# Attention scores as three products of rounded halves in place of one float32 product, with k split where it is transposed and q split tile by tile

## The chip, the cores and the metric

The kernel runs on one core of a Trainium2 chip. The metric is the device time of one execution in microseconds, as the median of several runs of the same program. The core has a matrix engine (PE, with its weight loads shown apart as PEld), three engines for elementwise work (DVE, ACT, POOL), and SP, which here only issues DMAs. Each engine works through its own list of instructions strictly in the order in which the program wrote them; engines wait for one another by semaphores.

## The reference

One encoder block over 1024 tokens of width 1024. The input projection feeds two groups: a gated depthwise convolution of 31 taps, and attention over a grid of 16 rows by 64 columns in which each query sees a clamped window of 8 rows by 16 columns. Then come an output projection, a residual, and a SwiGLU feed-forward network (FFN) with a residual. The change touches the scores alone:

```python
q = rms_norm(q.reshape(B, S, N_HEADS, HEAD_DIM), q_norm_g[l])   # 8 heads of 64
k = rms_norm(k.reshape(B, S, N_HEADS, HEAD_DIM), k_norm_g[l])
...
s = jnp.einsum("bqhd,brqchd->bhqrc", q_r, k_win,
               preferred_element_type=jnp.float32) * scale
s = s + bias
p = jax.nn.softmax(s, axis=(-2, -1))
```

## The kernel before

Almost every large matrix product is made from rounded halves. A float32 tile is split into a high part, its value rounded to a shorter mantissa (type `float32r`), and a low part, the difference. `split` writes the high part with a copy on ACT and the low part with a subtraction on another engine, by default POOL (lines 103 to 108). `mac` then adds three matmuls, high times high, high times low and low times high (lines 110 to 114). The attention is the exception: its scores (line 611), the transposes of the weights (642) and the products with v (658) are plain float32 matmuls.

The program is written out in the order in which each engine shall work. `weave` lets small pieces of work be written between the matmuls of a product, and `pump` writes convolution taps to DVE (line 319, some 1.3 us each) between other steps.

**The k stage.** `nat(1, t)` projects 128 tokens to k in the PSUM tile `z1t`. `head_post` follows it one step later: squares on ACT, then on DVE some taps, the reciprocal (line 380), the scaled copy `zn1t` (line 382), and one more tap. `head_T(1, t)` is written after the eighth triple of matmuls of the next projection: four transposes on PE (line 389), which read `zn1t`, then one ACT copy into `kT`, scaled by the norm's gain (line 396). So DVE has nothing to do for `kT` before the change. For tile 5 three taps more than usual stand ahead of the reciprocal (line 423). q goes the same way later, into `qT`.

**The attention loop** (lines 785 to 812) has 32 iterations for scores, each for a pair of heads of one tile of 128 queries; four in a row share a tile. The two heads of a pair lie in partitions 0 to 63 and 64 to 127 of `qT` and `kT`. Iterations 0 to 15 have windows of 288 keys, 16 to 31 windows of 384. In iteration i PE gets the scores of i (`score_mm`, tile `s`), the transposes of i - 2 (`flip`, tile `p`) and the product with v of i - 3 (`weigh`, tile `o`). DVE adds the bias and takes the maximum (624), ACT makes the exponentials and their sum (626), DVE the reciprocal (631). POOL scales the row of weights of iteration i - 1 (`score_norm`, line 633), which `flip` needs one iteration later. ACT and DVE copy the transposed weights out of the single PSUM buffer `p` (647). In eight iterations (16, 17, 20, 21, 24, 25, 28, 29) a quarter of an output weight is split as well, by an ACT copy (line 104) and a POOL subtraction (108), at the iteration's end; these are called jobs below. Iterations 0 and 1 lie between the last projections of v, beside the end of the convolution.

SBUF tiles come from pools with a fixed number of buffers: `H` holds six tiles of 16 KB per partition, `ST` five of 2 KB, `SM` sixteen small ones.

Of the kernel before, what the change touches and what calls it, by code (L numbers as in the profile page):

```python
# [6 lines left out]
F32 = mybir.dt.float32  # L7
F32R = mybir.dt.float32r
AF = mybir.ActivationFunctionType
OP = mybir.AluOpType  # L10
PSUM = bass.MemoryType.PSUM

P = 128
D = 1024
S = 1024
# [3 lines left out]
HD = 64  # L19
# [5 lines left out]
GW = 64  # L25
AR = 12
# [41 lines left out]
def build(ctx, tc, a):  # L68
    nc = tc.nc
    pe, act, dve, pool = nc.tensor, nc.scalar, nc.vector, nc.gpsimd  # L70
# [5 lines left out]
    def T(tag, shape, bufs, name, dt=F32):  # L76
        return sb.tile(shape, dt, tag=tag, bufs=bufs, name=name)
# [5 lines left out]
        return T("R", [P, 1024], 3, name)  # L83

    def H(name, dt=F32):
        return T("H", [P, 4096], 6, name, dt)

    def ST(name, dt=F32):
        return T("st", [P, 512], 5, name, dt)

    def SM(name, n=8):
        return T("sm", [P, 8], 16, name)[:, :n]

    def mm(name):
        return ps.tile([P, 512], F32, tag="mm", bufs=4, name=name)

    def tp(name):
        return ps.tile([P, 512], F32, tag="tp", bufs=2, name=name)
# [4 lines left out]
    def split(hi, lo, src, sub=(pool,)):  # L103
        act.copy(hi, src)  # L104
        n = src.shape[-1] // len(sub)
        for i, eng in enumerate(sub):
            sl = slice(i * n, (i + 1) * n)
            eng.tensor_tensor(*[w[..., sl] for w in (lo, src, hi.bitcast(F32))], OP.subtract)  # L108
# [47 lines left out]
    def take_parts(jobs, n=4, sub=pool):  # L156
        i = pos[1]
        hi, lo = chunks[i][2]()
        w = 1024 // n

        def part(o):
            sl = slice(o, o + w)
            split(hi[:, sl], lo[:, sl], raws[i][:, sl], (sub,))
            if o + w == 1024:
                raws.pop(i)
                issue()
        pos[1] += 1
        jobs.extend(lambda o=o: part(o) for o in range(0, 1024, w))
# [62 lines left out]
    qg, kg = par[:, 144:145], par[:, 145:146]  # L231
# [124 lines left out]
    def pump(n):  # L356
        for _ in range(n):
            if not next(conv, False):
                return


    qT, kT = H("qT").rearrange("p (c s) -> p c s", s=S), H("kT").rearrange("p (c s) -> p c s", s=S)

    def head_sq(n, t, z):
        sq, ss = ST(f"sq{n}{t}"), SM(f"s{n}{t}")
# [20 lines left out]
    def head_T(n, t, zn):  # L386
        pt = tp(f"zt{n}{t}")
        for c in range(4):
            pe.transpose(pt[:, c * P:(c + 1) * P], zn[:, c * P:(c + 1) * P], ident)
        if n == 0:  # L390
            q5 = qT.rearrange("p c (h b i j) -> p c h b i j", h=2, b=4, j=16)
            p5 = pt.rearrange("p (c i b j) -> p c i b j", c=4, i=2, j=16)
            for i in range(2):
                act.activation(q5[:, :, t // 4, :, 2 * (t % 4) + i, :], p5[:, :, i], AF.Copy, scale=qgs)
        else:
            act.activation(kT[:, :, t * P:(t + 1) * P], pt.rearrange("p (c s) -> p c s", s=P), AF.Copy, scale=kg)

    vd = dr.tile([S, 512], F32, name="vd")

# [175 lines left out]
    def table(rh, ty):  # L575
        n = AR * t1[ty].shape[-1]
        src = tf[rh, ty].rearrange("i j h c -> (i j) (h c)")
        if rh == 0 and ty == 0:
            parts = [(G(f"tab{k}")[:, :n * min(3, NH - 3 * k)], 3 * k) for k in range(3)]
        else:  # L580
            parts = [(H(f"tab{rh}{ty}")[:, :NH * n], 0)]
        heads = []
        for w, h0 in parts:
            nc.sync.dma_start(w, src[:, h0 * n:h0 * n + w.shape[-1]])
            heads += [w[:, o:o + n] for o in range(0, w.shape[-1], n)]
        return heads
# [4 lines left out]
    def load_vw(cb, g):  # L591
        c0, ncol, _ = WIN[cb]
        if g % 2 == 0:
            vwt[cb, g // 2] = G(f"vw{cb}{g}").rearrange("p (g d) -> p g d", d=512)
        vw[cb, g] = vwt[cb, g // 2][:4 * ncol, g % 2, :]
        nc.sync.dma_start(vw[cb, g], vd.rearrange("(r c) d -> r c d", c=GW)[g * 4:g * 4 + 4, c0:c0 + ncol, :])


    k4 = kT.rearrange("p c (r w) -> p c r w", w=GW)
    order = [(rh, cb) for cb in (0, 3, 1, 2) for rh in range(2)]  # L600
    tab, es, pTs, os_, at, sums, pp = {}, {}, {}, {}, {}, {}, {}

    def score_mm(i):
        s_, hp = divmod(i, 4)
        rh, cb = order[s_]
        t = rh * 4 + cb
        c0, ncol, _ = WIN[cb]
        out = []
        for hh in range(2):
            s = mm(f"s{i}{hh}")[:, :AR * ncol]  # L610
            pe.matmul(s, qT[hh * HD:(hh + 1) * HD, hp, t * P:(t + 1) * P],  # L611
                      k4[hh * HD:(hh + 1) * HD, hp, rh * 4:rh * 4 + AR, c0:c0 + ncol], start=True, stop=True)
            out.append(s)
        return out

    def score_exp(i, ss):
        s_, hp = divmod(i, 4)
        rh, cb = order[s_]
        n = AR * WIN[cb][1]
        e = es[i] = G(f"e{i}").rearrange("p (h n) -> p h n", h=2)[:, :, :n]  # L620
        rs = SM(f"rs{i}", 2)
        for hh in range(2):
            mx = SM(f"mx{i}{hh}", 1)
            dve.tensor_tensor_reduce(out=e[:, hh], in0=ss[hh], in1=tab[rh, cb][2 * hp + hh], scale=-1.0,  # L624
                                     scalar=3.0e38, op0=OP.add, op1=OP.min, accum_out=mx)
            act.activation(e[:, hh], e[:, hh], AF.Exp, bias=mx, scale=-1.0, accum_out=rs[:, hh:hh + 1])  # L626
        sums[i] = rs

    def score_norm(i):
        rs = sums.pop(i)  # L630
        dve.reciprocal(rs, rs)  # L631
        for hh in range(2):
            pool.tensor_scalar(es[i][:, hh], es[i][:, hh], rs[:, hh:hh + 1], 1.0, op0=OP.mult, op1=OP.mult)  # L633

    def flip(i):
        s_, hp = divmod(i, 4)
        m = 4 * WIN[order[s_][1]][1]
        pp[i] = cv(f"p{i}")
        for hh in range(2):
            pt = pp[i][:, hh * 512:hh * 512 + 384]  # L640
            for g in range(3):
                pe.transpose(pt[:m, g * P:(g + 1) * P], es[i][:, hh, g * m:(g + 1) * m], ident)  # L642
        pTs[i] = G(f"pT{i}").rearrange("p (n h q) -> p n h q", h=2, q=P)[:m, :3]

    def flip_out(i, hh):
        m = pTs[i].shape[0]
        (dve.tensor_copy, act.copy)[hh](pTs[i][:, :, hh], pp[i][:m, hh * 512:hh * 512 + 384].rearrange(  # L647
            "p (n q) -> p n q", q=P))

    def weigh(i):  # L650
        s_, hp = divmod(i, 4)
        rh, cb = order[s_]
        if hp == 0:
            os_[s_] = tp(f"o{s_}").rearrange("p (c q) -> p c q", c=4)
        for g in range(3):
            for hh in range(2):
                c = (2 * hp + hh) * HD
                pe.matmul(os_[s_][hh * HD:(hh + 1) * HD, hp], vw[cb, rh + g][:, c:c + HD], pTs[i][:, g, hh],  # L658
                          start=g == 0, stop=g == 2)

    def evac_hi(s_):
        rh, cb = order[s_]
        if rh == 0:
            at[cb] = [G(f"at{cb}{w}", F32R).rearrange("p (c t q) -> p c t q", c=4, t=2) for w in range(2)]
        act.copy(at[cb][0][:, :, rh], os_[s_])
# [12 lines left out]
    def load_window(cb):  # L678
        for g in range(4):
            load_vw(cb, g)  # L680

    for t in range(6):
# [5 lines left out]
        if t == 3:  # L688
            tab[1, 0] = table(1, 0)
            tab[0, 3] = table(0, 2)  # L690
    pump(200)
    act.activation(warm, eps, AF.Exp)
    s0 = score_mm(0)
    value(6)
    for g in range(3):
# [83 lines left out]
    def fill(*ks):  # L779
        if not acc0:  # L780
            act.activation(warm, eps, AF.Sqrt)
            acc0.append(mm("pj0"))
        proj(0, 0, acc0[0], ks)

    for i in range(2, 32 + 2):
        if i == 5:
            tab[0, 1] = tab[0, 2] = table(0, 1)
        if i == 9:
            tab[1, 1] = tab[1, 2] = table(1, 1)
        if i in (6, 12):  # L790
            load_window(i // 6)
        if i in (14, 22):
            take_parts(jobs)
        if i < 32:
            ss = score_mm(i)
        if i >= 32:
            fill(*((4, 5) if i == 32 else (6,)))
        if i < 33:
            score_norm(i - 1)
        flip(i - 2)  # L800
        flip_out(i - 2, 1)
        if i < 32:
            score_exp(i, ss)
        flip_out(i - 2, 0)
        if i > 2:
            weigh(i - 3)
            if i % 4 == 2:
                evac_hi(i // 4 - 1)
            elif i > 6 and i % 4 in (0, 3):
                evac_lo((i + 1) // 4 - 2, slice(0, 2) if i % 4 == 3 else slice(2, 4))  # L810
        if jobs and i % 4 < 2:
            jobs.pop(0)()
# [403 lines left out]
    for s, p in enumerate(SEQ):  # L1216
        for k in range(QF - 2):
            n = s * QF + k
# [21 lines left out]

# [12 lines left out]
```

## Time and profile before

| | |
|---|---|
| median of 3 runs | 1063.78 us (1063.1 to 1064.61) |
| the profiled execution, its own time | 1063.23 us |
| its span in the profile | 1061.5 us |
| busy: PE, DVE, ACT, POOL | 98%, 66%, 42%, 36% of the span |
| k stage (first and last copy into `kT`) | 31.6 to 91.3 us |
| attention loop (first and last score matmul) | 225.0 to 308.5 us |

Times inside the span are microseconds from its start. A row of the timeline gives the start, the length, the engine, the line and the operation, `out<-in` by the program's names, the number of merged instructions, and in brackets how long the engine had been idle and what ended that. A row of the chain of work that ended last gives start, length, engine, tile and line; what stands there has nothing to hide behind.

### The profile page before, as it was taken

Reading aid. Unit: us, or ns where it says so; the run is one execution under the profiler, and the core shown is the slowest. Engines: PE = TensorE matmul, PEld = TensorE weight load, DVE = VectorE, ACT = ScalarE, POOL = GpSimd, SP = SyncE. Lnnn points to the kernel's source line nnn. Section 1 sums busy time; section 2 is a strip of 40 time slices with the busy share of each in tenths; the row PEclk is TensorE's granted clock in tenths of the full one; section 3 lists DMA queues with packets and bytes.
Section 4 is the critical chain, followed back from the end, with each engine's and each line's share of the span. In section 5 each row is a group of like instructions: output and inputs, shape, how many; then the busy total and the mean of one; then the engine's idle time right before and its main releaser. Section 6 shows DMA issues by size and latency. Waiting matters only on the chain.

```text
span 1061.5 us, 14053 instructions
## 1 busy us (share of the span) xinstructions
PE 1045.5 (98%) x5068; PEld 847.8 (80%) x5068; DVE 703.9 (66%) x1055; ACT 450.9 (42%) x987; POOL 383.8 (36%) x301
## 2 busy tenths in 40 slices
PE   7999999999999999999999999999999999999997
PEld 6888888876667887788888888888888888888886
DVE  6788987877765257666465564564655567858883
ACT  6456347726766234532323223232233344433441
POOL 0126765523542302444554544545444200002310
PEclk9999999999999999999999999999999999999999
DMA  9416781245504422032322323232231597634541
GB/s 333 165 49 224 223 256 38 77 151 159 165 30 161 137 100 80 23 127 83 134 96 96 109 99 102 97 129 100 70 134 75 198 320 275 208 99 137 188 141 42
DMA packets 68245, 144.06 MB, mean 136 GB/s; under 512 B 12496, under 2 KB 21200, under 8 KB 67536
## 3 DMA queue, kind: packets, MB, share of 16 engines
q1 hardware_dynamic: 66336, 139.95, 39.2%
q10 hardware_dynamic: 1840, 3.22, 0.9%
q8 instruction: 40, 0.66, 0.3%
q14 instruction: 29, 0.24, 0.1%
HBM read 103.99 MB, written 44.76 MB: 140 GB/s over the span
## 4 chain that ended last, share of the span: by engine, by line
PE 92%; DVE 5%; ACT 1%; issue 0%; DMA 0%; SPq 0%; DVEq 0%; ACTq 0%
PE B L113 5%; PE B L114 5%; PE B L112 5%; PE D L112 4%; PE D L114 4%; PE D L113 4%; PE A L112 4%; PE A L113 3%; PE A L114 3%; PE z L112 3%; PE z L113 3%; PE z L114 3%; PE gl L114 3%; PE gl L112 3%; PE gl L113 3%; DVE cv L319 3%
## 5 line engine op out<-in xcount | busy, mean ns | idle before, releaser
L319 DVE SCALAR_TENSOR_TENSOR cv<-u,par,cv 128x1009 f32<-128x1009 f32 (+14 forms) x92 | 117.5, 1277 | 2.4
L345 POOL TENSOR_TENSOR pa<-pa,pr 128x1022 f32<-128x1022 f32 (+5 forms) x24 | 58.0, 2415 | 50.8 <-ACT pr L344 35.2
L104 ACT CAST op<-sr 128x512 fp32r<-128x512 f32 x77 | 47.7, 619 | 50.2 <-PE B2d L114 21.3
L108 DVE TENSOR_TENSOR op<-sr,op 128x512 fp32r<-128x512 f32 x77 | 58.2, 756 | 14.8 <-ACT op L104 14.8
L1036 DVE TENSOR_TENSOR g<-B,g 128x512 f32<-128x512 f32 x22 | 15.2, 690 | 79.0 <-PE B L114 79.0
L1208 POOL TENSOR_TENSOR ou<-ou,resm 128x512 f32<-128x512 f32 x8 | 13.1, 1651 | 142.7 <-ACT op L104 135.0
L1045 ACT ACTIVATE D<-D 128x512 f32<-128x512 f32 x22 | 12.8, 582 | 112.8 <-DVE D L1044 112.8
L1031 DVE TENSOR_TENSOR u<-B,g 128x512 f32<-128x512 f32 x22 | 15.2, 691 | 62.0 <-PE B L114 62.0
L104 ACT CAST op<-wd 128x512 fp32r<-128x512 f32 x66 | 40.9, 619 | 33.5 <-DVE wd L1123 18.6
L108 DVE TENSOR_TENSOR op<-wd,op 128x512 fp32r<-128x512 f32 x66 | 49.7, 753 | 3.0 <-ACT op L104 1.3
L889 DVE TENSOR_TENSOR ts<-gu,ts 128x512 f32<-128x512 f32 x44 | 51.0, 1159 | 0.8
L633 POOL TENSOR_SCALAR e<-e,rs 128x288 f32<-128x288 f32 (+1 forms) x64 | 34.1, 545 | 45.9 <-DVE rs L631 37.1
L1034 ACT ACTIVATE A<-A 128x512 f32<-128x512 f32 x20 | 11.6, 582 | 76.3 <-PE A L114 76.3
L626 ACT ACTIVATE e<-e,mx 128x288 f32<-128x288 f32 (+1 forms) x64 | 36.2, 569 | 7.3 <-DVE mx L624 7.3
L889 DVE TENSOR_TENSOR ts<-gu 128x512 f32<-128x512 f32 x22 | 33.6, 1528 | 0.0
L624 DVE CUSTOM_DVE_ANT_0 e<-s,tab 128x288 f32<-128x288 f32 (+1 forms) x64 | 29.9, 504 | 3.6 <-PE s L611 3.6
L642 PEld LDWEIGHTS p<-ident,e 128*96 128x96 f32 (+1 forms) x192 | 20.1, 133 | 15.0 <-issue 10.4
L372 ACT ACTIVATE sq<-z,r 128x64 f32<-128x64 f32 x96 | 28.6, 334 | 6.5 <-PE z L114 6.5
L642 PE MATMUL p<-ident,e 128*96 128x128 f32 (+1 forms) x192 | 27.6, 280 | 0.6 <-DVE pT L647 0.6
L658 PE MATMUL o<-pT,vw 96*64 96x128 f32 (+1 forms) x384 | 28.0, 281 | 0.0
L611 PE MATMUL s<-kT,qT 64*128 64x288 f32 (+1 forms) x128 | 27.5, 495 | 0.5 <-DVE mx L624 0.5
L344 ACT ACTIVATE pr<-u,par 128x1022 f32<-128x1022 f32 (+5 forms) x24 | 27.0, 1137 | 1.6 <-ACT vs L402 1.6
(1038 smaller groups left out, 3452.6 us busy)
## 6 DMA issues: line engine op xcount, KB each, us to landing
gu<-in_gu SPq DMA_DIRECT2D x44, 512.0 KB
sr<-sd SPq DMA_DIRECT2D x77, 256.0 KB
sd<-sd SPq DMA_DIRECT2D x22, 512.0 KB
wd<-in_wd SPq DMA_DIRECT2D x44, 256.0 KB
sd<-g SPq DMA_DIRECT2D x33, 256.0 KB
x<-in_x SPq DMA_DIRECT2D x16, 512.0 KB
xd<-x SPq DMA_DIRECT2D x8, 512.0 KB
resm<-xd SPq DMA_DIRECT2D x16, 256.0 KB
```

The costliest lines, as they stand in the source:

```text
L104: act.copy(hi, src)
L108: eng.tensor_tensor(*[w[..., sl] for w in (lo, src, hi.bitcast(F32))], OP.subtract)
L112: pe.matmul(acc, lh, rh, start=start, stop=False, skip_group_check=True)
L113: pe.matmul(acc, lh, rl, start=False, stop=False, skip_group_check=True)
L114: pe.matmul(acc, ll, rh, start=False, stop=stop, skip_group_check=True)
L319: dve.scalar_tensor_tensor(acc[:, o], uc[:, i], dwk[:, c, t:t + 1], acc[:, o], OP.mult, OP.add)
L345: pool.tensor_tensor(pa[:, o], pa[:, o], pr[:, o], OP.add)
L624: dve.tensor_tensor_reduce(out=e[:, hh], in0=ss[hh], in1=tab[rh, cb][2 * hp + hh], scale=-1.0, scalar=3.0e38, op0=OP.add, op1=OP.min, accu ...
L626: act.activation(e[:, hh], e[:, hh], AF.Exp, bias=mx, scale=-1.0, accum_out=rs[:, hh:hh + 1])
L633: pool.tensor_scalar(es[i][:, hh], es[i][:, hh], rs[:, hh:hh + 1], 1.0, op0=OP.mult, op1=OP.mult)
L642: pe.transpose(pt[:m, g * P:(g + 1) * P], es[i][:, hh, g * m:(g + 1) * m], ident)
L889: dve.tensor_tensor(o, l, r, OP.subtract)
```

## The change

`kT` becomes two `float32r` tiles, high and low. The ACT copy of `head_T` writes the high one; a new DVE instruction computes the low one from the same PSUM tile. A new function `q_split` splits the 128 queries of one tile, 512 elements in each partition, into two `ST` tiles with `split`, so with an ACT copy and a POOL subtraction. It is written twice ahead of the loop and then at the head of the iterations 4, 8, 12, 16, 20 and 24, each time for the tile whose scores begin four iterations later. `score_mm` issues three matmuls for each head in place of one, the two heads in turn. `H` gets a seventh buffer for the second `kT`; one `SM` buffer and a scratch area for DMAs that the kernel does not use are given up for it.

```diff
     def H(name, dt=F32):
-        return T("H", [P, 4096], 6, name, dt)
+        return T("H", [P, 4096], 7, name, dt)
...
     def SM(name, n=8):
-        return T("sm", [P, 8], 16, name)[:, :n]
+        return T("sm", [P, 8], 15, name)[:, :n]
...
-    qT, kT = H("qT").rearrange("p (c s) -> p c s", s=S), H("kT").rearrange("p (c s) -> p c s", s=S)
+    qT = H("qT").rearrange("p (c s) -> p c s", s=S)
+    kT = [H(f"kT{w}", F32R).rearrange("p (c s) -> p c s", s=S) for w in range(2)]
...
-            act.activation(kT[:, :, t * P:(t + 1) * P], pt.rearrange("p (c s) -> p c s", s=P), AF.Copy, scale=kg)
+            p4 = pt.rearrange("p (c s) -> p c s", s=P)
+            hi, lo = [w[:, :, t * P:(t + 1) * P] for w in kT]
+            act.activation(hi, p4, AF.Copy, scale=kg)
+            dve.scalar_tensor_tensor(lo, p4, kg, hi.bitcast(F32), OP.mult, OP.subtract)
...
+    def q_split(s_):
+        rh, cb = order[s_]
+        o = (rh * 4 + cb) * P
+        qs[s_] = [ST(f"q{s_}{w}", F32R).rearrange("p (c q) -> p c q", c=4) for w in range(2)]
+        split(*qs[s_], qT[:, :, o:o + P])
...
-        out = []
-        for hh in range(2):
-            s = mm(f"s{i}{hh}")[:, :AR * ncol]
-            pe.matmul(s, qT[hh * HD:(hh + 1) * HD, hp, t * P:(t + 1) * P],
-                      k4[hh * HD:(hh + 1) * HD, hp, rh * 4:rh * 4 + AR, c0:c0 + ncol], start=True, stop=True)
-            out.append(s)
+        out = [mm(f"s{i}{hh}")[:, :AR * ncol] for hh in range(2)]
+        for n, (qw, kw) in enumerate(((0, 0), (0, 1), (1, 0))):
+            for hh in range(2):
+                half = slice(hh * HD, (hh + 1) * HD)
+                pe.matmul(out[hh], qs[s_][qw][half, hp], k4[kw][half, hp, rh * 4:rh * 4 + AR, c0:c0 + ncol],
+                          start=n == 0, stop=n == 2, skip_group_check=True)
...
     pump(200)
+    q_split(0)
+    q_split(1)
     act.activation(warm, eps, AF.Exp)
...
+        if i % 4 == 0 and 4 <= i < 28:
+            q_split(i // 4 + 1)
         if i in (14, 22):
             take_parts(jobs)
```

Three places show how the instructions stand. The first is DVE in the k stage, around tile 4 and tile 5 (`r` is a reciprocal, `zn` the scaled copy, `cv` rows are convolution taps, `zt` the transposed tile). Before:

```order
L380 RECIPROCAL r14_661<-d14_657 128x8
L382 SCALAR_TENSOR_TENSOR zn14_663<-z14_572,r1_104,r14_661 128x512
L319 SCALAR_TENSOR_TENSOR cv0_598<-u0_535,par_85,cv0_598 128x1013
L319 SCALAR_TENSOR_TENSOR cv0_598<-u0_535,par_85,cv0_598 128x1014
L319 SCALAR_TENSOR_TENSOR cv0_598<-u0_535,par_85,cv0_598 128x1015
L319 SCALAR_TENSOR_TENSOR cv0_598<-u0_535,par_85,cv0_598 128x1016
L319 SCALAR_TENSOR_TENSOR cv0_598<-u0_535,par_85,cv0_598 128x1017
L319 SCALAR_TENSOR_TENSOR cv0_598<-u0_535,par_85,cv0_598 128x1018
L380 RECIPROCAL r15_723<-d15_716 128x8
L382 SCALAR_TENSOR_TENSOR zn15_725<-z15_616,r1_104,r15_723 128x512
```

The same stretch of DVE after the change:

```order
L381 RECIPROCAL r14_666<-d14_662 128x8
L383 SCALAR_TENSOR_TENSOR zn14_668<-z14_577,r1_104,r14_666 128x512
L319 SCALAR_TENSOR_TENSOR cv0_603<-u0_540,par_85,cv0_603 128x1013
L400 SCALAR_TENSOR_TENSOR kT1_107<-zt14_699,par_85,kT0_106 128x4x128
L319 SCALAR_TENSOR_TENSOR cv0_603<-u0_540,par_85,cv0_603 128x1014
L319 SCALAR_TENSOR_TENSOR cv0_603<-u0_540,par_85,cv0_603 128x1015
L319 SCALAR_TENSOR_TENSOR cv0_603<-u0_540,par_85,cv0_603 128x1016
L319 SCALAR_TENSOR_TENSOR cv0_603<-u0_540,par_85,cv0_603 128x1017
L319 SCALAR_TENSOR_TENSOR cv0_603<-u0_540,par_85,cv0_603 128x1018
L381 RECIPROCAL r15_729<-d15_722 128x8
L383 SCALAR_TENSOR_TENSOR zn15_731<-z15_621,r1_104,r15_729 128x512
```

The low half of k's tile 4 now stands after one tap, with five taps, the reciprocal and the scaled copy of tile 5 behind it.

The second place is POOL in the attention loop, from iteration 4 on (the rows with `e` are `score_norm`, two instructions each). Before:

```order
L633 TENSOR_SCALAR e4_2221<-e4_2221,rs4_2222 128x288 x2
L633 TENSOR_SCALAR e5_2254<-e5_2254,rs5_2255 128x288 x2
L633 TENSOR_SCALAR e6_2291<-e6_2291,rs6_2292 128x288 x2
L633 TENSOR_SCALAR e7_2325<-e7_2325,rs7_2326 128x288 x2
L633 TENSOR_SCALAR e8_2358<-e8_2358,rs8_2359 128x288 x2
```

The same stretch of POOL after the change:

```order
L643 TENSOR_SCALAR e4_2262<-e4_2262,rs4_2263 128x288 x2
L643 TENSOR_SCALAR e5_2299<-e5_2299,rs5_2300 128x288 x2
L643 TENSOR_SCALAR e6_2340<-e6_2340,rs6_2341 128x288 x2
L108 TENSOR_TENSOR q31_2396<-qT_105,q30_2395 128x512
L643 TENSOR_SCALAR e7_2378<-e7_2378,rs7_2379 128x288 x2
L643 TENSOR_SCALAR e8_2419<-e8_2419,rs8_2420 128x288 x2
```

The subtraction for a tile of q (here tile 3, in iteration 8) stands ahead of the scaling of the iteration before.

The third place is ACT in the same loop, in iterations 11 and 12 after the change (`pT` rows are copies of transposed weights, `e` rows exponentials, two for each iteration):

```order
L636 ACTIVATE e11_2528,rs11_2529<-e11_2528,mx110_2530 128x288
L636 ACTIVATE e11_2528,rs11_2529<-e11_2528,mx111_2533 128x288
L104 CAST q40_2551<-qT_105 128x512
L657 COPY pT10_2573<-p10_2566 96x3x128
L636 ACTIVATE e12_2575,rs12_2576<-e12_2575,mx120_2577 128x288
L636 ACTIVATE e12_2575,rs12_2576<-e12_2575,mx121_2580 128x288
```

The copy that makes the high half of q stands behind both exponentials of iteration 11; without it the copy of `pT10` followed them at once.

More of the change, by code (lines that the diff above doesn't have):

```diff
@@ L596, in load_vw @@
         nc.sync.dma_start(vw[cb, g], vd.rearrange("(r c) d -> r c d", c=GW)[g * 4:g * 4 + 4, c0:c0 + ncol, :])
-    k4 = kT.rearrange("p c (r w) -> p c r w", w=GW)
+    k4 = [w.rearrange("p c (r w) -> p c r w", w=GW) for w in kT]
+    qs = {}
+    def q_split(s_):
[3 more added lines that the diff above has]
+        split(*qs[s_], qT[:, :, o:o + P])
     order = [(rh, cb) for cb in (0, 3, 1, 2) for rh in range(2)]
@@ L605, in score_mm @@
         rh, cb = order[s_]
-        t = rh * 4 + cb
         c0, ncol, _ = WIN[cb]
-        out = []
-        for hh in range(2):
-            s = mm(f"s{i}{hh}")[:, :AR * ncol]
-            pe.matmul(s, qT[hh * HD:(hh + 1) * HD, hp, t * P:(t + 1) * P],
-                      k4[hh * HD:(hh + 1) * HD, hp, rh * 4:rh * 4 + AR, c0:c0 + ncol], start=True, stop=True)
-            out.append(s)
+        out = [mm(f"s{i}{hh}")[:, :AR * ncol] for hh in range(2)]
[4 more added lines that the diff above has]
+                          start=n == 0, stop=n == 2, skip_group_check=True)
         return out
@@ L1242 @@
     arrays = layout(inputs)
-    nc = bacc.Bacc("TRN2", target_bir_lowering=False, num_devices=1)
+    nc = bacc.Bacc("TRN2", target_bir_lowering=False, num_devices=1, dynamic_dma_scratch_size=64)
     aps, ins = {}, {}
```

## The prediction

> **What bounds the kernel now.** I read the page first, then PE's own waits, then the chain of waits that ended last, and in the stages of the change the timeline of each engine.
>
> ```profile
> PE 1045.5 (98%) x5068; PEld 847.8 (80%) x5068; DVE 703.9 (66%) x1055; ACT 450.9 (42%) x987; POOL 383.8 (36%) x301
> PE z L112 <- ACT wk0h L104: 6.5, 1, 6.5
> PE p L642 <- DVE pT L647: 0.6, 1, 0.6
> ```
>
> PE bounds nearly everything, and after its start it never waits as long as 1 us. So PE time saved is time won, and a wait put on PE is time lost. The attention loop in the chain, at 288 and at 384 keys:
>
> ```profile
> 254.80 0.69 PE s L611 x4
> 255.49 0.79 PE p L642 x6
> 256.28 0.81 PE o L658 x12
> ...
> 290.41 0.85 PE s L611 x4
> 291.26 0.81 PE p L642 x6
> 292.07 0.81 PE o L658 x12
> ```
>
> The three groups follow each other without a gap: an iteration is 2.29 and then 2.46 us of PE, and the scores are 0.69 and 0.85 of it.
>
> **Change, part 1: the low half of k on DVE.** Eight DVE instructions come in. The rows around tiles 4 and 5 of k, counted from 0:
>
> ```profile
> 72.37 0.44 PE zt L389 x4
> ...
> 78.12 0.60 PE L389 MATMUL zt<-ident,zn 128*128 128x128 f32 x4
> ...
> 72.84 0.69 ACT L396 ACTIVATE kT<-zt,par 128x512 f32<-128x512 f32 x1 [6.05 <-PE zt L389]
> ...
> 66.42 0.75 DVE L382 SCALAR_TENSOR_TENSOR zn<-z,r,r 128x512 f32<-128x512 f32 x1
> 67.09 7.85 DVE L319 SCALAR_TENSOR_TENSOR cv<-u,par,cv 128x1013 f32<-128x1013 f32 x6
> 76.26 0.20 DVE L380 RECIPROCAL r<-d 128x8 f32<-128x8 f32 x1 [1.32 <-ACT d L375]
> 76.57 0.75 DVE L382 SCALAR_TENSOR_TENSOR zn<-z,r,r 128x512 f32<-128x512 f32 x1
> ...
> 35.55 4.37 DVE L260 SCALAR_TENSOR_TENSOR hT<-xt,par,hT 128x512 fp32r<-128x512 f32 x4
> 41.78 2.73 DVE L260 SCALAR_TENSOR_TENSOR hT<-xt,par,hT 128x512 fp32r<-128x512 f32 x4
> ```
>
> Before, DVE runs six taps from 67.09 to 74.94, waits 1.32 us for ACT, and has `zn15` ready at 77.32, 0.8 us before PE transposes it at 78.12. Now the low half of tile 4 stands behind the first tap. It reads what ACT writes at 72.84 + 0.69 = 73.53, and ACT cannot be earlier, for the transposes end only at 72.8. So DVE stands still until about 73.6, with five taps, the reciprocal and `zn15` queued behind. Its own length is not in the trace: the same operation from SBUF takes 2.73 / 4 = 0.68 to 4.37 / 4 = 1.09, the one that also reads PSUM (line 382) 0.75. I take 0.75, the nearest in operands. Then 73.6 + 0.7 + 5 x 1.31 = 80.85; reciprocal and `zn15` start 0.3 later and end at 81.9; PE, ready at 78.12, starts at 81.95: **+3.8 us**, between 3.75 and 4.2.
>
> A second stall should not follow. From the transpose of tile 5 to that of tile 6 lie 5.9 us of projection; DVE then needs the ACT copy (0.7), the low half (0.75), only two taps (2.6), and 1.05 for reciprocal and copy, 5.2 with hand-overs. For tiles 0 to 3 the transposes lag their scaled copies much further, and the low halves delay DVE by 2 to 3 us between 50 and 60, where PE waits for nothing it makes. Is the loss won back later? Before the loop DVE ends the convolution in one unbroken run that starts behind the last tile of q, so behind PE:
>
> ```profile
> 201.90 28.89 DVE L319 SCALAR_TENSOR_TENSOR cv<-u,par,cv 128x1010 f32<-128x1010 f32 x22
> ```
>
> It moves with PE. Nothing wins it back.
>
> **Part 2: the score matmuls.** Four records are two heads times two passes. Rows for how they lie:
>
> ```profile
> 247.88 0.51 PE L611 MATMUL s<-kT,qT 64*128 64x288 f32 x2
> ...
> L611 PE MATMUL s<-kT,qT x128: 402/495/587, 225.0 to 308.0; 64*128 64x288 f32 x64, 64*128 64x384 f32 x64
> ```
>
> Two records begin within 0.01 us and fill 0.51, hardly more than one of them: the two heads run side by side. From 288 to 384 keys the group grows by 0.16, so two passes over 96 columns cost 0.16, or 0.83 ns a column. A pass over 288 is 0.24, the rest 0.69 - 0.48 = 0.21 is the change of operands at both ends. A rounded product passes 512 columns in (78.28 - 72.37 - 0.44) / 24 = 0.228 (24 matmuls lie between the two `zt` of the chain, the first quoted above, the second here):
>
> ```profile
> 78.28 0.44 PE zt L389 x4
> ```
>
> That is 0.445 ns a column: 0.128 and 0.171 per pass; with the excess over 0.417 ns taken as fixed, 0.135 and 0.175. Three passes at 0.13 and 0.172 give 0.21 + 0.39 = 0.60 and 0.205 + 0.515 = 0.72, a gain of 0.09 and 0.125. It counts in 14 iterations of the first kind (PE waits after iteration 0 for DVE's convolution and after iteration 3 for the 0.6 us quoted above, so these two gain nothing) and 16 of the second: **-3.3 us**. The ends are -4.4 (0.417 ns a column, no extra) and, were the heads of a rounded product one after the other, six passes: +0.30 and +0.39 an iteration, +10.4. I stay at the first, since the heads do run side by side now. The Trainium skill (TensorEngine Tiling, Key Properties) says that tiles are independent and load weights and multiply in parallel; the float32 rows agree at 0.51 us for two, and no row here shows it for rounded halves. By that rule the term is the one taken.
>
> **Part 3: the split of q.** The first two lie ahead of the loop and cost nothing: ACT makes the high halves from 220.7 and POOL is free after 219; the scores need both at 225.
>
> ```profile
> 216.59 2.39 POOL L345 TENSOR_TENSOR pa<-pa,pr 128x1017 f32<-128x1017 f32 x1 [2.86 <-ACT pr L344]
> 219.65 0.69 ACT L402 ACTIVATE vs<-z,r 128x512 f32<-128x512 f32 x1 [3.20 <-PE z L114]
> ```
>
> If that cover failed, PE would wait up to 2 us. The other six stand in the loop, on POOL ahead of the scaling that the next `flip` waits for:
>
> ```profile
> 253.08 0.19 ACT L626 ACTIVATION_READ_ACCUMULATOR e<-e,mx 128x1 f32 x1
> 253.66 0.98 POOL L633 TENSOR_SCALAR e<-e,rs 128x288 f32<-128x288 f32 x2 [1.35 <-DVE rs L631]
> 254.09 0.47 ACT L647 COPY pT<-p 96x384 f32<-96x384 f32 x1 [0.82 <-PE p L642]
> 255.42 0.31 PE L642 MATMUL p<-ident,e 128*96 128x128 f32 x1
> ...
> 291.19 0.19 ACT L626 ACTIVATION_READ_ACCUMULATOR e<-e,mx 128x1 f32 x1
> 293.65 0.33 PE L642 MATMUL p<-ident,e 128*128 128x128 f32 x1
> ...
> 271.39 0.19 ACT L626 ACTIVATION_READ_ACCUMULATOR e<-e,mx 128x1 f32 x1
> 274.00 0.32 PE L642 MATMUL p<-ident,e 128*96 128x128 f32 x1
> ...
> L104 ACT CAST op<-sr 128x512 fp32r<-128x512 f32 x77 | 47.7, 619 | 50.2 <-PE B2d L114 21.3 <-DMA sr<-sd 13.5 <-issue 12.9
> L108 POOL TENSOR_TENSOR t10m<-ts,t10m 128x512 fp32r<-128x512 f32 x4 | 5.2, 1291 | 9.7 <-ACT t10m L104 9.7
> L108 POOL TENSOR_TENSOR t9m<-gu,t9m 128x512 fp32r<-128x512 f32 x3 | 4.4, 1452 | 0.0
> ```
>
> In iteration 8 ACT ends the exponentials of 7 at 253.27. The high half is ready 0.53 later (0.62, begun 0.09 before the end of the last, as casts here do), POOL starts 0.08 after that, subtracts 1.29 (1.45 at the other end), scales 0.98, and PE follows 0.04 later: 256.19. PE, two shorter scores earlier than in the row, is ready at 255.42 - 0.18 = 255.24. Stall 0.95, in iterations 4, 8 and 12. In 20 and 24: 291.38 + 0.53 + 0.08 + 1.29 + 1.15 + 0.04 = 294.47 against 293.65 - 0.25, so 1.07. In 16: 271.58 + 2.92 = 274.50 against 273.75, so 0.75. Together 2.85 + 2.14 + 0.75 = **+5.7 us**; 6.7 with 1.45. ACT itself is not late: it waits 0.82 us for the next `p` there, longer than the high half takes.
>
> **Part 4: the jobs.** In their eight iterations POOL already ends as PE arrives:
>
> ```profile
> 285.08 1.15 POOL L633 TENSOR_SCALAR e<-e,rs 128x384 f32<-128x384 f32 x2
> 286.27 0.64 PEld L642 LDWEIGHTS p<-ident,e 128*128 128x128 f32 x6 [0.54 <-POOL e L633]
> PEld p L642 <- POOL e L633: 4.4, 8, 0.5
> ```
>
> From `flip` to the `flip` two later runs a path over ACT and POOL that fills two periods of 2.46. With two of 2.33 PE waits some 0.25, once for each of the four pairs, the second of a pair or the first being covered: **+0.9 us**. H, SM and the scratch area move no work onto the path; the seventh H buffer can only free a tile sooner, in stages where PE waits for none: 0.
>
> **Sum.** +3.8 - 3.3 + 5.7 + 0.9 = +7.1 us against the profiled execution: 1063.23 (span 1061.5 and 1.7 around it) becomes 1070.3. The median of the runs is 0.55 higher, so 1070.9.
>
> **Rivals.**
> (a) The new stall cools PE. At the start PE works after 6.5 us of rest:
>
> ```profile
> 8.29 0.63 PE L112 MATMUL z<-wk0h,hT 128*128 128x512 f32 x1
> 9.56 0.63 PE L112 MATMUL z<-wk0h,hT 128*128 128x512 f32 x1
> ```
>
> These are three matmuls apart, 0.42 each, not 0.228. Eight such (an estimate: up to 10 us of the span no other pace shows) would add 1.6 us, 1072.5, if 3.8 us of rest are enough. No gap between 0.9 and 6.5 is there to tell. The Trainium skill (TensorE: Matmul & The Clock Gate, Why this matters for your kernels) warns of gaps over about 3 us, which would then run at half clock; its rule speaks for this rival.
> (b) PE does not overlap as before: weights loaded between passes (0.107 more a pass, from 0.21 / 2 at each end of a group) give +0.23 and +0.20 an iteration, with shorter stalls some 1075.9; heads one after the other 1078.
> (c) Part 1 does not reach PE, because DVE is earlier than I read: 1067.1.
> (d) POOL's split is hidden, for instance by a faster subtraction: 1063.23 + 3.8 - 3.3 + 0.55 = 1064.3, no change.
> (e) Both hidden, the gain alone: 1060.5, faster. It decides where DVE finds `zt14` done when it comes to it and POOL needs under 0.3 us for 512 elements; rows for both speak against it.
>
> **Chances.** Forecast 0.50; (a) 0.13; (b) 0.13; (c) 0.08; (d) 0.07; (e) 0.09. About 0.2% is what a measurement here tells from no change: 2.1 us. Slower by more: forecast, (a), (b), (c), 0.84; within: (d), 0.07; faster: (e), 0.09. The range 1066.5 to 1076 holds the forecast with its ends (-4.4, 1.45), (a), (c) and half of (b), 0.78. For the forecast alone it is 1069.5 to 1072.5.
>
> **What would show it.** Right: in the changed trace PE waits once for 3 to 4 us ahead of the transposes of k's tile 5, for DVE's `zn`; DVE stands some us before the low half of tile 4; the scores fill about 0.60 and 0.72; weight loads of `p` wait for POOL's scaling about 1 us in iterations 4, 8, 12, 16, 20, 24; the FFN's spacing is unchanged. Wrong: scores longer than 0.69, or no wait of PE near 78 us, or half-speed matmuls after it.

## The result, and the profile after

The changed kernel takes 1070.07 us (median of 6 runs, 1067.28 to 1071.79) against 1063.24 us for the kernel before, run beside it (6 runs, 1062.38 to 1064.61). The ratio is 1.0059, with a 95% interval from 1.0049 to 1.007: slower, by 6.8 us, where 1070.9 was forecast. The profiled execution is the fastest of the six: 1067.28 us, span 1065.6, mean granted clock 0.999 (the share of its full clock that PE was given). The other five took 1069.73 to 1071.79 at a clock of 0.996 or 0.997. That difference is part of the answer and is taken up below.

First the busy times of the page and PE's own waits (line waited for, then total us, times, longest):

```profile
PE 1043.2 (98%) x5132; PEld 852.0 (80%) x5132; DVE 709.1 (67%) x1063; ACT 455.2 (43%) x995; POOL 393.9 (37%) x309
PE zt L390 <- DVE zn L383: 3.5, 1, 3.5
PE p L652 <- DVE rs L641: 1.3, 3, 0.4
PE p L652 <- POOL e L643: 0.9, 3, 0.4
```

PE is busy for 2.3 us less than before and the span is 4.1 us longer: the matmuls did get cheaper, and waits ate more than that. The six short waits stand ahead of the six `flip`s that come behind a split of q. Three of them are put down to DVE's reciprocal, but the weight loads of the same transposes wait for POOL's scaling in all six. The long wait has its place in the timeline, at tile 5 of k:

```profile
71.75 0.60 PE L390 MATMUL zt<-ident,zn 128*128 128x128 f32 x4
72.38 0.69 ACT L399 ACTIVATE kT<-zt,par 128x512 fp32r<-128x512 f32 x1 [3.54 <-PE zt L390]
73.11 0.75 DVE L400 SCALAR_TENSOR_TENSOR kT<-zt,par,kT 128x512 fp32r<-128x512 f32 x1 [2.71 <-ACT kT L399]
73.77 6.54 DVE L319 SCALAR_TENSOR_TENSOR cv<-u,par,cv 128x1014 f32<-128x1014 f32 x5
80.22 0.20 DVE L381 RECIPROCAL r<-d 128x8 f32<-128x8 f32 x1
80.45 0.75 DVE L383 SCALAR_TENSOR_TENSOR zn<-z,r,r 128x512 f32<-128x512 f32 x1
81.35 0.63 PE L390 MATMUL zt<-ident,zn 128*128 128x128 f32 x4 [3.53 <-DVE zn L383]
```

DVE stands idle for 2.71 us before the low half of tile 4 (line 400), the five taps, the reciprocal and the scaled copy follow it back to back, and PE waits 3.53 us for that copy. From tile 4 to tile 5 PE takes 9.60 us. Before the change it is 5.91, from this row to the one at 78.12 us:

```profile
72.21 0.60 PE L389 MATMUL zt<-ident,zn 128*128 128x128 f32 x4
```

In the loop, the chain of work that ended last:

```profile
246.46 0.59 PE s L622 x6
...
249.62 1.01 PE p L652 x6
250.64 0.81 PE o L668 x12
251.44 0.59 PE s L622 x6
...
292.10 0.73 PE s L622 x6
```

The scores fill 0.59 and 0.73 us, before 0.69 and 0.85. The transposes `p` of the weights of iteration 3, whose scaling stands behind the split of q in iteration 4, are stretched to 1.01 us; the timeline shows why:

```profile
247.81 1.28 POOL L108 TENSOR_TENSOR q<-qT,q 128x512 fp32r<-128x512 f32 x1 [1.33 <-ACT q L104]
...
249.06 1.96 POOL L643 TENSOR_SCALAR e<-e,rs 128x288 f32<-128x288 f32 x4
...
249.62 0.28 PEld L652 LDWEIGHTS p<-ident,e 128*96 128x96 f32 x3 [0.61 <-POOL e L643]
...
250.10 0.28 PEld L652 LDWEIGHTS p<-ident,e 128*96 128x96 f32 x3 [0.20 <-POOL e L643]
```

POOL subtracts, then scales. One scaling of both heads is two instructions of 0.49 us each (the 1.96 us row holds four, two iterations' worth). PE starts the three transposes of the first head at 249.62, 0.07 us after the first of them has ended, waits 0.20 us for the second, and does the other three. It never waited for the whole scaling. From the flip of iteration 0 (its first transpose, at 242.66 us) to that of 31 (317.74 us) the loop takes 75.08 us, before 74.27 (239.58 to 313.85 us).

### The profile page after: what moved, and what is told of

The parts are those of the page before. It is cut to its first block, busy times and chain, and to the rows that moved or that the text cites. A ratio compares the mean times of both kernels' runs of the same rounds, so it can differ in the third digit from the quotient of the medians.

```text
span 1065.6 us, 14199 instructions
## 1 busy us (share of the span) xinstructions
PE 1043.2 (98%) x5132; PEld 852.0 (80%) x5132; DVE 709.1 (67%) x1063; ACT 455.2 (43%) x995; POOL 393.9 (37%) x309
## 4 chain that ended last, share of the span: by engine, by line
PE 89%; DVE 6%; ACT 3%; issue 1%; POOL 1%; DMA 0%; SPq 0%; ACTq 0%; DVEq 0%; POOLq 0%
PE B L113 5%; PE B L114 5%; PE B L112 5%; PE D L113 4%; PE D L114 4%; PE D L112 4%; PE A L112 3%; PE A L113 3%; PE A L114 3%; DVE cv L319 3%; PE z L112 3%; PE z L113 3%; PE z L114 3%; PE gl L112 3%; PE gl L114 3%; PE gl L113 3%
## 5 line engine op out<-in xcount | busy, mean ns | idle before, releaser
L954 POOL TENSOR_TENSOR xn<-xn,xn 128x512 f32<-128x512 f32 x4 | 6.9, 1731 | 56.9 <-DVE sn L954 56.9
```

## The experiments

All ratios are to the kernel before on the same chip, with their 95% interval.

**The changed kernel again, and its two halves moved.** The theory at this point: two stalls that depend on where the splits stand on DVE and POOL, and a loss of clock behind the first. One kernel is the changed one unaltered. One writes the low half of k behind the next tile's scaled copy ("k late"), one the split of q behind the scaling ("q late"), one does both.

> The changed kernel once more, unaltered. Theory 1 (a wait of 3.5 us on PE near 78 us sometimes cools its clock, by chance of where a fixed window falls): the runs spread as the first six did, 1067 to 1072, the granted clock of the long ones is 0.996 or 0.997 and that of the short ones 0.999, and a trace of a long one shows matmuls 0.42 apart behind that wait. Theory 2 (the spread comes from DMAs or from the loop): clock and time do not go together, and no matmul after 10 us is at half speed. Time against before by both: 1.005 to 1.007.

1069.78 us (1068.71 to 1070.68), ratio 1.0061 (1.0049 to 1.0074), at clocks of 0.996 to 0.998. Its profiled execution was a slower one, and its trace has a stretch at half clock that the first trace has not. The timeline of PE behind the stall, and further on:

```profile
82.46 1.09 PE L390 MATMUL zt<-ident,zn 128*128 128x128 f32 x4 [3.53 <-DVE zn L383]
...
84.20 0.63 PE L114 MATMUL gl<-hT,ag11l 128*128 128x512 f32 x1
84.63 0.63 PE L112 MATMUL gl<-hT,ag11h 128*128 128x512 f32 x1
...
88.34 0.39 PE L112 MATMUL gl<-hT,ag11h 128*128 128x512 f32 x1
88.56 0.39 PE L113 MATMUL gl<-hT,ag11h 128*128 128x512 f32 x1
```

Right behind the wait the matmuls follow each other every 0.43 us, later every 0.22 to 0.23. The trace also records when the granted clock changes: it is halved at 81.77 us and full again 3.413 us later. From tile 5 to tile 6 PE takes 7.24 us here, 5.95 in the first trace: 1.3 us. A start-up wait that the first trace has not (1.1 us, PE for POOL's split of a weight, near 33 us) makes up most of the rest of the 2.5 us between the two.

```diff
-            dve.scalar_tensor_tensor(lo, p4, kg, hi.bitcast(F32), OP.mult, OP.subtract)
+            lows.append(lambda: dve.scalar_tensor_tensor(lo, p4, kg, hi.bitcast(F32), OP.mult, OP.subtract))
...
+        while lows:          # in step(), behind the head_post of the next tile
+            lows.pop(0)()
```

> The low half of a tile of k is written behind the scaled copy of the next tile in DVE's list; all else as in the changed kernel. Theory 1: no wait of PE at the transposes of tile 5, the clock back at 0.999 in every run, so 3.7 us of the wait and some 2 to 3 us of slow clock are gone: 1063.5 to 1064.5, within 0.1% of before, with little spread. Theory 2 (the wait alone): 1066.4 and the spread stays. Theory 3 (the loss lies in the buffers or elsewhere): 1069 to 1070.

1065.18 us (1064.34 to 1066.63), ratio 1.0021 (1.0012 to 1.0029). The wait at tile 5 is gone (5.91 us from tile 4 to tile 5), the clock stays full there, and 4.6 us are won. The time is still some 0.7 us above what was expected, for PE has a new wait:

```profile
PE rb L289 <- DVE kT L400: 0.9, 1, 0.9
```

Low halves that wait hold the PSUM buffer of their transposes, and the transposes of `rb` take theirs from the same two buffers.

```diff
-        if i % 4 == 0 and 4 <= i < 28:
-            q_split(i // 4 + 1)
...
         if i < 33:
             score_norm(i - 1)
+        if i % 4 == 0 and 4 <= i < 28:
+            q_split(i // 4 + 1)
```

> The split of a tile of q is written behind score_norm instead of ahead of it, so POOL scales first and subtracts then; all else as in the changed kernel. By the trace of the changed kernel the six stalls cost 3.7 us (pitch of the transposes 0.37 to 0.69 longer), so 1066.3 at the median and the spread of the clock stays. By the prediction's price (5.7 for the stalls): 1064.4. If POOL's subtraction did not cost PE anything: no change, 1070.

1066.71 us (1065.39 to 1067.8), ratio 1.0033 (1.002 to 1.0045): 3.1 us less than the changed kernel. No flip waits for POOL any more. The wait at tile 5 and a half-clock stretch behind it are still there; tile 5 to tile 6 takes 7.52 us. The loop takes 72.54 us, with one new wait of 1.2 us in it.

> Both moves together. Theory 1: what is left is the shorter scores, 3.2 us less than before, perhaps 0.2 of late scaling in the job iterations: 1060.0 to 1060.6, ratio 0.997, clock 0.999. If the score groups did not gain on the path: 1063.

1062.88 us (1061.91 to 1063.74), ratio 0.9995 (0.9986 to 1.0004). The stalls of both parts are gone, and the clock stays full. The time stays 2.3 us or more above what was expected: a wait of 1.3 us ahead of `rb`, and the new one in the loop.

**Where those two waits come from.** The second showed as PE waiting for DVE's copy of `p` at iteration 19's flip. DVE was late since its first instruction on the last bias table had to wait; the view of waits names POOL, and the timeline of DVE and of SP's queue in the kernel with q's split late says this:

```profile
287.13 0.56 DVE L634 CUSTOM_DVE_ANT_0 e<-s,tab 128x384 f32<-128x384 f32 x1 [1.45 <-POOL e L643]
...
252.09 17.88 SPq L600 DMA_DIRECT2D vw<-vd  x4
270.07 2.39 SPq L588 DMA_DIRECT2D tab<-tf  x1
```

The table (1536 KB) stands behind four loads of v on SP's queue, and those fill 18 us there. In a loop without stalls, the theory went, the scores reach it before it has landed.

```diff
+            low = lambda: dve.scalar_tensor_tensor(lo, p4, kg, hi.bitcast(F32), OP.mult, OP.subtract)
+            lows.append(low) if t > 3 else low()      # and q's split behind the scaling, as above
```

> The changed kernel with the low half of k written at once for tiles 0 to 3 and behind the next tile's scaled copy for tiles 4 to 7, and with q's split behind the scaling. Theory: the kernel with all eight low halves late still had a wait of 1.3 us of PE for DVE's low half ahead of the rows of r, because two of them hold PSUM buffers; with tiles 0 to 3 at once it goes, and no wait at tile 5 comes back: 1062.9 - 1.3 = 1061.6, clock 0.998 or over. Rival that the early low halves delay DVE at tile 4 or 5 anyway: a wait of 1 us or more at a zt, 1062.9 or more.

1061.57 us (1060.85 to 1063.42), ratio 0.9983 (0.9974 to 0.9992): as expected, and faster than the kernel before. The wait ahead of `rb` is gone; 0.2 us is back at tile 5 (6.11 us from tile 4 to tile 5).

```diff
-        if i in (6, 12):
-            load_window(i // 6)
+        if i in (10, 12):
+            load_window(1 if i == 10 else 2)
```

> As the other with both late, and the loads of v's window 1 issued in iteration 10, so behind the last bias table, in place of iteration 6, ahead of it. Theory: in the loop with q's split late the one wait left, 1.1 to 1.2 us ahead of the flip of iteration 19, is DVE's wait for the last table's transfer, which stands behind those loads on SP's queue; with the order exchanged it goes: 1.1 us less than the other, 1060.5, and the loop flows at 2.19 and 2.34 us. Rival that it is POOL's scaling that DVE waits for, as the view of waits infers: no change, 1061.6. Rival that the window then comes too late: a wait ahead of the first weighing of iteration 16, 1 us or more.

1060.34 us (1059.8 to 1061.5), ratio 0.9969 (0.9956 to 0.9981). The wait of DVE's copy falls from 2.1 us in two waits to one of 0.7; in PE's waits, first of the kernel with the loads as they were:

```profile
PE p L655 <- DVE pT L660: 2.1, 2, 1.4
```

then of the one with the loads moved:

```profile
PE p L655 <- DVE pT L660: 0.7, 1, 0.7
```

and SP's queue of the latter, in the timeline, has the tables first:

```profile
246.59 6.73 SPq L591 DMA_DIRECT2D tab<-tf  x3
253.43 24.32 SPq L603 DMA_DIRECT2D vw<-vd  x8
```

So it was the transfer, not POOL. From flip 0 to flip 31 the loop now takes 71.28 us, 3.0 less than before the change. This version beats both kernels: the arithmetic of the change is worth 3 us once nobody waits for its splits or for that table.

**The price of q's split alone.** Only tiles 4 to 7 of k late, q's split where the change has it.

> The changed kernel with tiles 4 to 7 of k late alone; q's split stays ahead of the scaling. Theory: six stalls of 0.37 to 0.69 us, 3.7 us in all, as in the changed kernel, since a flip waits for the scaling of its first head alone; from the flip of iteration 0 to that of 31 75.1 us, against 72.7 with q's split late and 71.3 with the last table's load early as well; 1060.3 + 3.8 = 1064.1. Rival, the price of the prediction (a flip waits for both heads): 5.7 + 0.9 us of stalls, 1066.9.

1064.38 us (1063.56 to 1065.33), ratio 1.0007 (0.9997 to 1.0016), and the loop takes 75.04 us. The split's place costs 3.8 us of loop against the version above (1064.38 - 1060.34 = 4.0 us in the medians), not 5.7 + 0.9. That version also has the loads of v moved. With them where they were the loop takes 72.68 us, and the difference is 2.4 us: the wait for the table comes out once the stalls are gone.

**How long a rest costs clock.** Two kernels that have nothing of the change. They only repeat DVE's scaled copy for tile 5 of k, so that PE rests there.

```diff
+        if (n, t) == (1, 5):
+            for _ in range(4):          # 8 in the second kernel
+                dve.scalar_tensor_tensor(...)      # zn once more
```

> The kernel before with nothing of the change, but DVE computes the scaled copy of k's tile 5 four times more (0.75 us each by its row, or a little less back to back), so the only effect is a wait of PE ahead of the transposes of that tile: 2.8 to 3.0 us of DVE work less the 0.8 us that it was early, 2.0 to 2.2 us. Theory that a rest of about 3.4 us or more costs clock: a rest of 2.1 us is too short, no half-clock window behind it, tile 5 to tile 6 stays 5.95 us, and the time is the kernel before plus 2.1, 1065.3. Rival that the clock has nothing to do with the rest: 1065.3 too. Rival that any rest of over 1 us cools PE: 1066.7 and a half-clock window.

> As the one with four, with eight more: 5.6 to 6.0 us of DVE work, a wait of PE of 4.8 to 5.2 us. Theory that a rest of 3.4 us or more costs clock: a window of about 3.4 us at half clock behind it in the profile and in nearly every execution, tile 5 to tile 6 at 7.3 to 7.6 us in place of 5.95, the time 1063.2 + 5.0 + 1.5 = 1069.7. Rival that the clock has nothing to do with the rest, and the excess of the changed kernel over its fastest run comes from elsewhere: 1068.2, tile 5 to tile 6 at 5.95.

With four: 1066.6 us (1065.89 to 1067.17), ratio 1.0026 (1.0016 to 1.0037), a rest of 2.3 us. The eight times lie in two groups, four from 1065.89 to 1066.31 and four from 1066.90 to 1067.17; the profiled one, 1067.12, has a half-clock stretch and takes 7.52 us from tile 5 to tile 6. With eight: 1071.35 us (1070.59 to 1071.93), ratio 1.0072 (1.0059 to 1.0085), a rest of 5.5 us, half clock for 6.83 us, 7.55 us from tile 5 to tile 6. So my threshold of 3.4 us was wrong, and so was the other end. A rest of 2.3 us cooled PE (cost it half its clock for a stretch) in the traced execution, and one of 3.5 us left it warm in the first trace of the changed kernel. The rival that any rest of over 1 us cools PE had 1066.7 us, but the traces above have waits of 1.3 us (ahead of `rb`, both late) and of 1.4 (in the loop, v's loads not yet moved) with the clock full behind them.

The traces say what decides. In all of them the granted clock changes at multiples of 3.413 us counted from when it first became full, at 10.1 to 12.3 us in these four. Laid on that grid, the stretches around the rest (start and end, us, then busy time and instructions of PE, PEld, DVE, ACT, POOL, the granted clock, the DMAs' share and rate) are, in the changed kernel run again:

```profile
78.35:81.77 3.42, 0.58 (x3) 0.16 (x1) 3.31 (x5) 0.52 (x1) 3.42 (x2) 1.00 0.67 180
81.77:85.18 3.41, 2.72 (x9) 2.36 (x10) 2.61 (x4) 1.59 (x8) 0.96 (x1) 0.50 1.01 395
85.18:88.59 3.41, 3.41 (x17) 2.78 (x16) 3.34 (x5) 2.80 (x12) 0.43 (x1) 1.00 0.78 285
```

In its first profiled execution, the one of 1067.28 us:

```profile
76.27:79.69 3.42, 1.55 (x7) 0.94 (x5) 3.31 (x4) 1.48 (x2) 2.73 (x2) 1.00 0.39 54
79.69:83.10 3.41, 1.75 (x10) 1.57 (x11) 3.03 (x5) 1.09 (x5) 1.93 (x1) 1.00 0.74 265
83.10:86.51 3.41, 3.41 (x17) 2.80 (x16) 3.34 (x5) 3.31 (x16) 0.00 (x0) 1.00 1.02 399
```

In the kernel with four copies more:

```profile
77.04:80.46 3.42, 1.10 (x5) 0.58 (x4) 3.28 (x6) 1.03 (x2) 3.18 (x2) 1.00 0.71 241
80.46:83.87 3.41, 3.40 (x10) 2.88 (x11) 3.34 (x3) 2.27 (x13) 1.50 (x1) 0.50 1.02 404
```

And with eight:

```profile
77.12:80.53 3.41, 1.31 (x6) 0.75 (x4) 3.27 (x5) 1.24 (x2) 2.96 (x2) 1.00 0.72 208
80.53:83.95 3.42, 0.03 (x1) 0.07 (x1) 3.28 (x6) 0.00 (x0) 1.70 (x1) 0.50 1.02 406
83.95:87.36 3.41, 3.41 (x10) 2.83 (x11) 3.34 (x3) 2.32 (x13) 0.00 (x0) 0.50 0.64 229
87.36:90.77 3.41, 3.41 (x16) 2.82 (x15) 2.40 (x5) 2.08 (x8) 1.15 (x1) 1.00 0.45 97
```

A stretch in which PE was busy for 0.03, 0.58, 1.10 or 1.31 us is followed by one at half clock; one with 1.55 or 1.75 is not. Other traces agree: 0.68 us behind the wait of the kernel with q late, half clock; and at the kernels' ends 1.38 us (k late, 1055.35 to 1058.76 us), half clock, and 1.56 us (both late, 1053.90 to 1057.31 us), full clock. The same wait of 3.53 us falls into one stretch in the second trace (2.8 us of it) and is cut in two in the first (1.86 and 1.66), and only the former cools.

With a bound of 1.31 to 1.55 us busy, so 1.86 to 2.10 us idle, a wait of 3.5 us escapes only where the border cuts it with neither part above the bound: for 0.2 to 0.7 us of the grid's 3.41, or an estimated 6% to 21% of executions. Of the eleven of the changed kernel, the one at a clock of 0.999 did; one at 0.998 can't be told, for the kernel before has 0.998 as well. A wait of 2.3 us would be caught in 44% to 58%. The two groups of four would fit, and so do their clocks (0.998 to 0.999, and 0.996 to 0.998), but they overlap, and only one of the eight has a trace.

The Trainium skill (TensorE: Matmul & The Clock Gate, Part 1: The HAM clock gate) gives the window as 3413 ns and free-running; the stretches agree with both. It also says that the clock drops after an idle window, and there these rows differ: a window with 1.31 us of work in it was enough.

**The heads in another order.** To see whether the two heads overlap because the code takes them in turn, the three products of one head were written ahead of the three of the other:

```diff
-        for n, (qw, kw) in enumerate(((0, 0), (0, 1), (1, 0))):
-            for hh in range(2):
+        for hh in range(2):
+            for n, (qw, kw) in enumerate(((0, 0), (0, 1), (1, 0))):
```

> As the kernel with tiles 4 to 7 of k late (q's split where the change has it), with the three products of one head ahead of the three of the other, in place of the heads taking turns. Theory that the two heads run side by side only while they take turns: one product of each still overlaps, five passes instead of three, a group of 6 takes 0.85 and 1.06 us in place of 0.60 and 0.73, and the time is about 8 to 9 us above 1065.2 less 0.9, so 1073. Rival that the pairs overlap whatever the order: groups of 0.60 and 0.73, 1064.3. Rival that they never overlapped and the products are just cheap: no change either, and the records' starts follow each other.

The kernel that ran also had q's split behind the scaling, which the text above has wrong: its figures are to be set beside 1061.57, not 1064.3. It took 1061.61 us (1060.54 to 1062.42), ratio 0.9981 (0.9972 to 0.999): no difference. Three rows of PE's timeline, cut off a little later each time in the same group (260.60, 260.80, 260.95 us):

```profile
260.52 0.40 PE L625 MATMUL s<-kT,q 64*128 64x288 f32 x2
...
260.52 0.54 PE L625 MATMUL s<-kT,q 64*128 64x288 f32 x4
...
260.52 0.67 PE L625 MATMUL s<-kT,q 64*128 64x288 f32 x6
```

The six records still begin in pairs, and a group still fills 0.60 us (the next one, `p`, starts at 261.12). In PE's list of instructions, as built from this kernel, the products stand 3 + 3, and the signals that tell of a finished score stand on the third and the sixth; in the trace they stand on the last two to begin, at 260.89 and 260.90. So the second head's products start before the first head's are through.

**One buffer fewer.** Behind the loop, from the first transposes of the convolution to those of its tile 7, every kernel with the change takes 14.71 to 14.73 us, before 14.36. The kernel before with `SM` at 15 buffers:

> The kernel before with 15 small buffers in place of 16 and nothing else of the change. From the first transposes of the convolution behind the loop to those of its tile 7 the kernel before takes 14.36 us, every kernel with the change 14.72 to 14.73. Theory: the small buffer given up makes a statistic of one tile wait for an earlier one there, so 14.7 here. Rival: it comes from the change in the loop ahead of it, 14.36 here. Time 1063.2 to 1063.7 by either.

14.71 us there, so it is the buffer: 0.35 us. The two kernels with a longer rest, which keep sixteen buffers, take 14.38 and 14.39 us. (It ran once. That time, 1065.1 us, is over what was expected, and has a start of 8.1 us in place of 6.5 ahead of the first matmul.)

## Why the prediction was right, and what in it was not

The sign and the two stalls came out as forecast, but not each by the size given. The time did too, and in part by luck: two terms were too high, and two effects that the sum put at nothing, the clock and the small buffer, made up for them. One of the prediction's own signs of being wrong also came, half-speed matmuls behind the wait near 78 us.

- **Part 1, the low half of k: +3.8, measured +3.7.** DVE's idle time ahead of the low half, its length of 0.75 us, the five taps behind it and the one wait of PE (3.53 us) are the rows that were worked out. Nothing wins the time back, and late low halves take it away.
- **Part 2, the scores: -3.3, measured -3.0.** Groups of 0.59 and 0.73 against 0.60 and 0.72 forecast, and 74.27 - 71.28 us in the loop once no split stalls it. The heads run side by side.
- **Part 3, the split of q: +5.7, measured 3.7.** The place, the subtraction (1.28 us against 1.29) and the queue behind it were right. The step that failed is "scales 0.98, and PE follows 0.04 later": it priced the scaling of both heads as one thing. A flip starts after the first head's 0.49 us, and the second overlaps its first three transposes, at the price of some stretching: they take 1.01 us at 249.62, and 0.86 in an iteration without a split. 0.95 - 0.49 + 0.15 is 0.61, and the three stalls priced at 0.95 cost 0.61 to 0.67 us; all six cost 0.39 to 0.69. They fall one iteration behind the six splits, in 5, 9, 13, 17, 21 and 25.
- **Part 4, the jobs: +0.9, measured about 0.1.** The loop runs at 2.34 us through the job iterations where no split stalls it. That this is the same mistake (with only half the scaling ahead of the flip there is slack) is argued, not shown by a run of its own.
- **Rival (a), the clock: given 0.13, and by the granted clocks it happens in most executions.** A half-clock stretch costs 1.3 to 1.6 us, as (a) had it (1.6). It was weighed as if a length of rest decided, for want of a rest between 0.9 and 6.5 us; the rest's place on the clock's grid decides as well.
- **The buffers at 0: measured +0.35,** by the small buffer given up.

In sum: 3.7 - 3.0 + 3.8 + 0.35 is 4.9 us, 1068.1 for an execution at full clock. The profiled one is 0.8 us below that, of which 0.46 us is an earlier tile 4 of k. With 1.3 to 1.6 us of clock it is 1069.4 to 1069.7, where the medians are 1070.07 and 1069.78. So the 2.8 us by which parts 3 and 4 were priced too high stood in for the clock, the buffer, what part 2 fell short and the rest; that the sum came out is luck. The last 0.1 to 0.7 us stay open; waits of PE for POOL in the start-up that come and go between executions (0.9 to 1.1 us in two of the traces) would do for it, and were not tested. In the second trace of the changed kernel PE reaches the transposes of tile 1 of k at 38.30 us, before at 37.64; 0.7 us is as much.

Of the other rivals, (b) fell with the groups of 0.59 and 0.73, (c) and (d) with the two stalls, and (e) turned real only where both splits were moved.

## What to carry to other kernels

What splitting an operand cost here was set by what stands behind the split in its engine's queue: moving both splits behind the next urgent instruction, and one group of loads with them, turned 6.8 us lost into 3 us won. Price a wait by the first instruction that the waiter needs, not by the whole step that produces it. When a stall is gone, look at the DMA queues and buffers next: here a table's load and a held PSUM buffer came up one after the other.

## What was not expected of the hardware

- PE's clock was judged in fixed stretches of 3.413 us: with 1.38 us of work or less in one, the next ran at half speed; with 1.55 or more it did not. A wait of 2.3 us cost 1.6 us more in the execution that was traced, and the same wait of 3.5 us cost 1.3 us more in one trace and nothing more in another.
- Matmuls on the two halves of PE's rows did not keep the program's order among each other: written 3 + 3, they still began in pairs 0.01 us apart. So PE did not work through its list strictly in order there, as the opening has it of every engine.
